# A decoder layer on one core: input projections in native fp32, rotation's angles made first, memory keys and values in three passes of float32r

## The chip, the cores and the metric

The kernel runs on one core of one Trainium2 chip. The metric is device time in microseconds from one launch, lower is better. Three runs of the kernel before took 1092.56, 1095.22 and 1095.38 us (median 1095.22). Its five engines are named as in the profile: PE is TensorE's matmul, PEld its weight load, DVE is VectorE, ACT is ScalarE, POOL is GpSimd, and SP is the engine whose queue issues the loads.

## What is computed

One layer of a decoder on 256 tokens of width 1024, all in float32. Cut to what matters here:

```python
hn   = rmsnorm(x, mix_norm_g)
proj = hn @ w_in                     # 1024 x 2328: conv_a, conv_b, q, six k/v parts, gate logits
y_conv = silu(layernorm(conv31(conv_a * sigmoid(conv_b))))   # 31 taps per channel
q_r, k_s, k_w = partial_rope(...)    # rotation by cos and sin of positions * inv
y_nsa  = gated sum of compressed, selected and window attention
h  = x + concat(y_conv, y_nsa) @ w_out
k, v = rmsnorm(mem) @ w_mem_k, rmsnorm(mem) @ w_mem_v        # 256 memory rows
h  = h + softmax_attention(rmsnorm(h) @ w_mem_q, k, v) @ w_mem_o
h  = h + peer(rmsnorm(h))            # 16384 experts, top 16 of each of 8 heads
out = rmsnorm(h, final_norm_g)
```

## The kernel before

**Two ways to multiply float32.** In the first (`mm3`, lines 147 to 150) both operands are split into a high part of type float32r and the rest, also float32r, and three matmuls are summed: high by high, high by low, low by high. A weight chunk of 128 by 1024 is loaded into a `raw` buffer (`wload`, four buffers) and split there by `wsplit`: two ACT copies `hi` of 128x512 (line 137) and two DVE subtractions `lo` (line 138), with six `hi` and six `lo` buffers, that is, three chunks' worth. In the second way one matmul reads the float32 operands as they are. It needs no split, and the trace shows it as two matmul records.

**The stages in PE's order.** PE's instructions stand in the order of the program; the other engines' order is made by a planner that takes, at each simulated moment, the earliest instruction of the program that is ready, so that ready work is pulled ahead where an engine would be idle.

1. Input projections of the convolution (lines 286 to 309): for four channel blocks a chunk `pb` and a chunk `pa`, eight contraction steps each, by three float32r passes. `hx_h` and `hx_l` are x times the norm's gain, split. The norm's factor is found beside it: ACT squares, DVE sums (`r0.add`), PE adds over partitions (`ss_x`), DVE makes the inverse root in some 14 small steps, PE spreads it as a row (`sr_x`). Until that row is there, no `pb` or `pa` can be read out, and four PSUM buffers hold them. `conv_in` then makes u, and 31 taps per block (124 in all, line 271 and 273) run on DVE; `conv(n)` puts n of them at a place of the program.
2. The positions are loaded and the angles of the rotation are made: ten steps on DVE (lines 318 to 339), two sines on ACT.
3. Two chunks `pkv`, six chunks `pq` (with the rotation, one small permuting matmul `rp` each), and four chunks `pv` of 280 columns (lines 345 to 421). The memory's rows are loaded, scaled (`mg`, line 367), and their norm is made.
4. Attention (lines 471 to 668). Sixteen units of scores, softmax and transposes stand in PE's order with a filler between them: `fill(n)` takes n steps from a generator that makes the memory's keys (`pmk`, line 442, 64 steps) and values (`pmv`, line 458, 64 steps), each step one native float32 matmul. Before the unit of n = 13 ends, 106 of the 128 steps are used; there PE needs the sum of all convolution outputs (`lsum`, made by DVE after the last tap) for the layer norm's mean, `pmu` (line 619).
5. The output projection, memory attention, the search of the experts, and the two large expert products (from line 673), which the change doesn't touch.

Of the kernel before, what the change touches and what calls it, by code (L numbers as in the profile page):

```python
# [9 lines left out]
F32 = mybir.dt.float32  # L10
# [23 lines left out]
_n = 0  # L34
for _name, _w in (("mix_g", 8), ("memq_g", 8), ("memkv_g", 8), ("peer_g", 8), ("conv_w", 4 * TAPS),
                  ("conv_b", 4), ("ln_g", 4), ("ln_b", 4), ("cmp_b1", 2), ("cmp_b2k", 1),
                  ("cmp_b2v", 64), ("cmp_pos", 32)):
    PC[_name] = (_n, _n + _w)
    _n += _w
NPAR = _n  # L40
# [1 line left out]
CC = {}  # L42
_n = 0
for _name, _w in (("ident", 128), ("iota", 128), ("iota16", 16), ("perm", 128), ("causal", 128), ("cmp_add", 32),
                  ("cmp_mul", 32), ("rsel", 512), ("inv", 1), ("sgn", 1)):
    CC[_name] = (_n, _n + _w)
    _n += _w
NCON = _n
# [3 lines left out]
def constants():  # L52
    c = np.zeros((P, NCON), np.float32)

    def put(name, v):
        a, b = CC[name]
        c[:, a:b] = v

    p = np.arange(P)
    put("ident", np.eye(P))  # L60
    d = p % 64
    sw = np.where(d < 8, p + 8, p - 8)
    perm = np.zeros((P, P), np.float32)
# [22 lines left out]
    inv = (np.float32(500000.0) ** (-(np.arange(8, dtype=np.float32) * np.float32(2.0) / np.float32(16.0)))).astype(np.float32)  # L86
    put("inv", np.where(d < 16, inv[d % 8], 0.0)[:, None])
    put("sgn", np.where(d < 8, -1.0, np.where(d < 16, 1.0, 0.0))[:, None])
    put("iota16", np.broadcast_to(cc[None, :], (P, 16)))
    return c  # L90


def build(tc, A, out, dbg=None):
# [19 lines left out]
    def Pm(name):  # L113
        return par[:, PC[name][0]:PC[name][1]]
# [123 lines left out]
    nc.sync.dma_start(xT[:, 0:2], A["xT"][:, 0:2])  # L238
    nc.sync.dma_start(par, A["par"])
    w0 = wload(A["w_in_t"][0])  # L240
    for q in range(1, 4):
        nc.sync.dma_start(xT[:, 2 * q:2 * q + 2], A["xT"][:, 2 * q:2 * q + 2])


    hx_h = h2p.tile([P, KC, T], F32R, name="hx_h", tag="act_h")
    hx_l = h2p.tile([P, KC, T], F32R, name="hx_l", tag="act_l")
    hx = (hx_h, hx_l)
    r0 = Rstd("x", pool=ch, eng=V)
    w0 = wsplit(w0)
    for k in range(KC):  # L250
        g = Pm("mix_g")[:, k:k + 1]
        if k in (1, 2, 3, 4, 5, 6, 7):
            S.activation(hx_h[:, k], xT[:, k], AF.Copy, scale=g)
        else:
            V.tensor_scalar(hx_h[:, k], xT[:, k], g, None, op0=ALU.mult)
        V.scalar_tensor_tensor(hx_l[:, k], xT[:, k], g, hx_h[:, k].bitcast(F32), op0=ALU.mult, op1=ALU.subtract)


    u = ch.tile([P, 4, 30 + T], F32, name="u")
# [26 lines left out]
    pend = []  # L286
    for i in range(4):
        pb = psum(T, f"pb{i}")
        wb = wchunk(A["w_in_t"][2 * i]) if i else w0
        proj(pb, wb, hx, range(4))  # L290
        if i == 1:
            r0.sums()
        proj(pb, wb, hx, range(4, KC))
        wa = wchunk(A["w_in_t"][2 * i + 1], None)
        if i == 0:
            for k in range(KC):
                r0.add(xT[:, k])
# [13 lines left out]
    posi = wk.tile([P, T], I32, name="posi", tag="rt")  # L311
    nc.sync.dma_start(posi, A["pos"].partition_broadcast(P))


    Ct = ch.tile([P, T], F32, name="Ct")
    St = ch.tile([P, T], F32, name="St")
    posf = wk.tile([P, T], F32, name="posf", tag="tb")
    V.tensor_copy(posf, posi)
    ang = wk.tile([P, T], F32, name="ang", tag="th")
    V.tensor_scalar(ang, posf, C("inv"), None, op0=ALU.mult)  # L320
    kk = wk.tile([P, T], F32, name="kk", tag="ta")
    MAGIC = 12582912.0
    V.tensor_scalar(kk, ang, 1.0 / (2.0 * math.pi), None, op0=ALU.mult)
    V.tensor_scalar(kk, kk, MAGIC, None, op0=ALU.add)
    V.tensor_scalar(kk, kk, MAGIC, None, op0=ALU.subtract)
    c1 = 6.28125
    c2 = float((np.array([2.0 * math.pi - c1], np.float32).view(np.uint32) & np.uint32(0xFFFFF000)).view(np.float32)[0])
    c3 = 2.0 * math.pi - c1 - c2
    for c in (c1, c2, c3):
        V.scalar_tensor_tensor(ang, kk, -c, ang, op0=ALU.mult, op1=ALU.add)  # L330
    PIF = 3.1415925
    V.tensor_scalar(ang, ang, PIF, -PIF, op0=ALU.min, op1=ALU.max)
    halfpi = cst.tile([P, 1], F32, name="halfpi")
    V.memset(halfpi, math.pi / 2)
# [778 lines left out]
def layout(inp):  # L1113
# [11 lines left out]
        np.broadcast_to(b2[1][None, :], (P, 64)), pos_l], axis=1))  # L1125
# [48 lines left out]
```

## Time and profile before

| | before |
|---|---|
| median of three runs | 1095.22 us |
| the profiled execution's own time | 1095.67 us |
| its span, first to last instruction | 1093.9 us |
| outside the span | 1.8 us |
| granted TensorE clock, mean of the span | 0.990 |
| busy: PE, PEld, DVE, ACT, POOL | 1066.3, 980.1, 877.1, 587.6, 102.0 us |

Matmuls overlap in the pipeline, so a busy PE is read by the distance between starts and not by the duration of one record. In the table of windows the columns are: stretch in us, its length, then for PE, PEld, DVE, ACT and POOL the busy time with the number of instructions, then the granted clock (1.00 is 2.4 GHz, half of it 1.2 GHz), the share of the DMA engines and GB/s. In a timeline they are start, duration, engine, line, operation, output and inputs, shapes, count, and in brackets the idle time before it and what ended that.

### The profile page before, as it was taken

The numbers are of one execution on the slowest core, as the hardware profiler recorded it, in microseconds if no ns is written. First come the engines' busy times: TensorE is split into PE (matmuls) and PEld (weight loads), VectorE is DVE, ScalarE is ACT, GpSimd is POOL, SyncE is SP. The second block draws the span as 40 slices with busy tenths as digits, with TensorE's granted clock in tenths as the row PEclk, the third lists the DMA queues.
The fourth block names the chain that finished last, engine by engine and source line by source line (L and its number), as shares of the span: only waits on it lengthen the run. The fifth ranks groups of instructions, "written<-read, shape, count | busy, mean of one in ns | idle before, by whom it ended". The sixth has DMA issues, their size and how long they took to land.

```text
span 1093.9 us, 20604 instructions
## 1 busy us (share of the span) xinstructions
PE 1066.3 (97%) x7361; PEld 980.1 (90%) x7362; DVE 877.1 (80%) x2229; ACT 587.6 (54%) x1349; POOL 102.0 (9%) x82
## 2 busy tenths in 40 slices
PE   8889999999999999999999999999999999999997
PEld 7878878999999999999999999998888888888885
DVE  6998956988779999788899999996666666666665
ACT  5731446656445555665555555455555555555554
POOL 0000000000027994000000000001000000000000
PEclk9899999999999999999999999999999999999999
DMA  8633224644444564555544455456665665555652
GB/s 272 215 100 106 88 78 135 203 144 136 155 154 139 171 198 147 184 167 160 167 158 155 158 169 157 155 182 206 194 196 195 193 195 193 195 194 193 194 192 79
DMA packets 51687, 182.47 MB, mean 167 GB/s; under 512 B 5760, under 2 KB 6528, under 8 KB 51456
## 3 DMA queue, kind: packets, MB, share of 16 engines
q1 hardware_dynamic: 51296, 180.62, 50.7%
q8 instruction: 58, 0.95, 0.4%
q10 hardware_dynamic: 288, 0.52, 0.1%
q14 instruction: 45, 0.37, 0.1%
HBM read 179.81 MB, written 1.05 MB: 165 GB/s over the span
## 4 chain that ended last, share of the span: by engine, by line
PE 83%; DVE 14%; ACT 1%; issue 1%; DMA 1%; SPq 0%; ACTq 0%; DVEq 0%
PE Y L1074 32%; PE pu L148 9%; PE pu L150 8%; PE pu L149 8%; PE pmk L442 3%; PE pmv L458 2%; PE pw L1020 1%; PE ppq L148 1%; PE ppq L149 1%; PE ppq L150 1%; PE pw L1021 1%; DVE lo L138 1%; DVE ohx L951 1%; DVE ohx L949 1%; PE pmw L149 1%; PE pmw L148 1%
## 5 line engine op out<-in xcount | busy, mean ns | idle before, releaser
L137 ACT ACTIVATE hi<-raw 128x512 fp32r<-128x512 f32 x632 | 380.1, 624 | 179.0 <-PE pu L149 67.1
L138 DVE TENSOR_TENSOR lo<-raw,hi 128x512 fp32r<-128x512 f32 (+1 forms) x564 | 372.6, 683 | 27.4 <-ACT hi L137 21.5
L148 PE MATMUL pu<-hn_h,hi 128*128 128x256 f32 x1024 | 296.0, 289 | 0.0
L150 PE MATMUL pu<-hn_h,lo 128*128 128x256 f32 x1024 | 290.4, 284 | 1.9 <-DVE lo L138 1.9
L149 PE MATMUL pu<-hn_l,hi 128*128 128x256 f32 x1024 | 290.3, 284 | 0.0
L150 PEld LDWEIGHTS pu<-hn_h,lo 128*128 128x128 f32 x1024 | 197.0, 192 | 2.1 <-DVE lo L138 2.1
L149 PEld LDWEIGHTS pu<-hn_l,hi 128*128 128x128 f32 x1024 | 197.2, 193 | 0.0
L148 PEld LDWEIGHTS pu<-hn_h,hi 128*128 128x128 f32 x1024 | 197.1, 192 | 0.0
L1074 PE MATMUL Y<-hi,ah 128*128 128x512 f32 x512 | 158.2, 389 | 0.0
L1074 PE MATMUL Y<-hi,al 128*128 128x512 f32 x512 | 158.1, 389 | 0.0
L1074 PE MATMUL Y<-lo,ah 128*128 128x512 f32 x512 | 158.0, 389 | 0.0
L1074 PEld LDWEIGHTS Y<-lo,ah 128*128 128x128 f32 x512 | 96.1, 188 | 19.9
L1074 PEld LDWEIGHTS Y<-hi,al 128*128 128x128 f32 x512 | 96.1, 188 | 19.9
L1074 PEld LDWEIGHTS Y<-hi,ah 128*128 128x128 f32 x512 | 96.1, 188 | 19.9
L158 DVE TENSOR_TENSOR al<-slB,ah 128x256 fp32r<-128x256 f32 x88 | 37.4, 425 | 86.1 <-PE Y L1074 86.1
L157 ACT ACTIVATE ah<-slB 128x256 fp32r<-128x256 f32 x88 | 36.8, 418 | 110.7 <-PE Y L1074 110.7
L138 POOL TENSOR_TENSOR lo<-raw,hi 128x512 fp32r<-128x512 f32 x68 | 94.5, 1417 | 12.6 <-ACT hi L137 10.1
L1026 ACT ACTIVATE slB<-pw 128x348 f32<-128x348 f32 (+31 forms) x64 | 32.5, 507 | 70.4 <-DVE slB L1025 58.9
L273 DVE SCALAR_TENSOR_TENSOR yc<-u,par,yc 128x256 f32<-128x256 f32 x120 | 56.0, 478 | 0.3
L158 DVE TENSOR_TENSOR al<-slA,ah 128x256 fp32r<-128x256 f32 x40 | 17.6, 440 | 36.9 <-PE Y L1074 36.9
L157 ACT ACTIVATE ah<-slA 128x256 fp32r<-128x256 f32 x40 | 16.7, 418 | 49.3 <-PE Y L1074 48.0
L148 PE MATMUL ppq<-gx_h,hi 128*128 128x256 f32 x128 | 37.3, 292 | 0.0
(387 smaller groups left out, 1768.8 us busy)
## 6 DMA issues: line engine op xcount, KB each, us to landing
raw<-u SPq DMA_DIRECT2D x128, 512.0 KB, 3.4
raw<-v SPq DMA_DIRECT2D x128, 512.0 KB, 4.3
raw<-peer_w_q SPq DMA_DIRECT2D x16, 512.0 KB, 3.4
raw<-w_in_t SPq DMA_DIRECT2D x15, 512.0 KB, 4.6
raw<-w_mem_k SPq DMA_DIRECT2D x8, 512.0 KB, 3.5
raw<-w_mem_v SPq DMA_DIRECT2D x8, 512.0 KB, 3.4
raw<-w_out SPq DMA_DIRECT2D x8, 512.0 KB, 3.8
raw<-w_mem_q SPq DMA_DIRECT2D x8, 512.0 KB, 4.3
```

Source lines behind the costliest of these rows:

```text
L137: S.activation(hi, r, AF.Copy)
L138: (engs or (V, V))[q].tensor_sub(lo, r, hi.bitcast(F32))
L148: PE.matmul(ps, w[0], xh, start=start, stop=False)
L149: PE.matmul(ps, w[0], xl, start=False, stop=False)
L150: PE.matmul(ps, w[1], xh, start=False, stop=stop)
L157: S.activation(dst[0], src, AF.Copy)
L158: V.tensor_sub(dst[1], src, dst[0].bitcast(F32))
L273: V.scalar_tensor_tensor(yc[:, i], u[:, i, j:j + T], w, yc[:, i], op0=ALU.mult, op1=ALU.add)
L442: PE.matmul(ps, wr[:, k * P:(k + 1) * P], mg[:, k], start=(k == 0), stop=(k == KC - 1))
L458: PE.matmul(pss[hf], mg[:, k, sl], wr[:, j * 256:(j + 1) * 256], start=(k == 0), stop=(k == KC - 1))
L1026: S.activation(slB[:, done - J:, n0:n0 + 4].rearrange("p i n -> p n i"), pw[:, :, done:], AF.Copy, scale=1.0 / GSC)
L1074: PE.matmul(Y[nh][c], lhs[:, sl], wc[c][t], start=False, stop=i == KEYS - 1 and lhs is a[1], skip_group_check=True)
```

## The change

The sixteen input chunks and the four `pv` chunks are multiplied in native float32 from the raw weights and one tile `hx` (no `hx_l`, no split of these weights). The angles' constants move to the parameters that are loaded first, the load of the positions moves ahead of the rest of x in SP's queue, and the angles are made on DVE ahead of the convolution, with one multiply-and-add fused and the sign put into the sine's scale; the two sines stay behind the loop over the blocks. The memory's keys and values are multiplied in three float32r passes, with split weights and a split `mg`. The place of `r0.rows()` moves from behind six contraction steps of `pa` to behind four.

```diff
+    def proj1(ps, w, x, ks=range(KC)):
+        for k in ks:
+            PE.matmul(ps, w[0][:, k * P:(k + 1) * P], x[:, k], start=k == 0, stop=k == KC - 1)
...
+    posi = wk.tile([P, T], I32, name="posi", tag="rt")
+    nc.sync.dma_start(posi, A["pos"].partition_broadcast(P))
     for q in range(1, 4):
         nc.sync.dma_start(xT[:, 2 * q:2 * q + 2], A["xT"][:, 2 * q:2 * q + 2])
-    hx_h = h2p.tile([P, KC, T], F32R, name="hx_h", tag="act_h")
-    hx_l = h2p.tile([P, KC, T], F32R, name="hx_l", tag="act_l")
+    hx = h2p.tile([P, KC, T], F32, name="hx", tag="act_h")
     for k in range(KC):
-            S.activation(hx_h[:, k], xT[:, k], AF.Copy, scale=g)
...
-        V.scalar_tensor_tensor(hx_l[:, k], xT[:, k], g, hx_h[:, k].bitcast(F32), op0=ALU.mult, op1=ALU.subtract)
+        V.tensor_scalar(hx[:, k], xT[:, k], Pm("mix_g")[:, k:k + 1], None, op0=ALU.mult)
+        r0.add(xT[:, k])
+    V.tensor_copy(posf, posi)
+    V.tensor_scalar(ang, posf, Pm("inv"), None, op0=ALU.mult)
+    V.tensor_scalar(kk, ang, 1.0 / (2.0 * math.pi), MAGIC, op0=ALU.mult, op1=ALU.add)
+    V.tensor_scalar(kk, kk, MAGIC, None, op0=ALU.subtract)
...
+    V.scalar_tensor_tensor(aabs, ang, -1.0, ang, op0=ALU.mult, op1=ALU.max)
...
-        wb = wchunk(A["w_in_t"][2 * i]) if i else w0
-        proj(pb, wb, hx, range(4))
+        wb = wload(A["w_in_t"][2 * i]) if i else w0
+        proj1(pb, wb, hx)
         if i == 1:
             r0.sums()
-        proj(pb, wb, hx, range(4, KC))
-        wa = wchunk(A["w_in_t"][2 * i + 1], None)
+        wa = wload(A["w_in_t"][2 * i + 1])
-        proj(pa, wa, hx, range(6))
+        proj1(pa, wa, hx, range(4))
         if i == 1:
             r0.rows()
...
-    S.activation(St, ang, AF.Sin)
-    V.tensor_scalar(St, St, C("sgn"), None, op0=ALU.mult)
+    S.activation(St, ang, AF.Sin, scale=Pm("sgn"))
+    S.activation(Ct, aabs, AF.Sin, scale=-1.0, bias=halfpi)
-        proj(ps, wchunk(A["w_in_t"][8 + i]), hx)
+        proj1(ps, wload(A["w_in_t"][8 + i]), hx)
...
-        proj(ps, wchunk(A["w_in_t"][10 + i]), hx)
+        proj1(ps, wload(A["w_in_t"][10 + i]), hx)
-    mg = mp.tile([P, KC, T], F32, name="mg", tag="b8c")
+    mg = mp.tile([P, KC, T], F32R, name="mg", tag="b8c")
+    mg_l = mp.tile([P, KC, T], F32R, name="mg_l", tag="b8d")
-        S.activation(mg[:, k], mT[:, k], AF.Copy, scale=Pm("memkv_g")[:, k:k + 1])
+        gain_split(mg[:, k], mg_l[:, k], mT[:, k], Pm("memkv_g")[:, k:k + 1])
-        wc = wsplit(wload(A["w_in_v"][w], 560), (V, V), 280, 280)
+        wc = wload(A["w_in_v"][w], 560)[0]
-            wr = wload(A["w_mem_k"][i])[0]
+            wc = wchunk(A["w_mem_k"][i])
-                PE.matmul(ps, wr[:, k * P:(k + 1) * P], mg[:, k], start=(k == 0), stop=(k == KC - 1))
+                proj(ps, wc, (mg, mg_l), [k])
                 yield
-                wr = wload(A["w_mem_v"][c, w])[0]
+                wc = wchunk(A["w_mem_v"][c, w], width=256)
-                        PE.matmul(pss[hf], mg[:, k, sl], wr[:, j * 256:(j + 1) * 256], start=(k == 0), stop=(k == KC - 1))
+                        PE.matmul(pss[hf], mg[:, k, sl], wc[j][0], start=(k == 0), stop=False)
+                        PE.matmul(pss[hf], mg[:, k, sl], wc[j][1], start=False, stop=False)
+                        PE.matmul(pss[hf], mg_l[:, k, sl], wc[j][0], start=False, stop=(k == KC - 1))
                         yield
```

## Rows read from the trace of the kernel before

**Rows 1.** Windows, the stretches from the start to the output projection.

```profile
0.00:24.90 24.90, 20.31 (x128) 18.89 (x129) 17.23 (x52) 14.29 (x30) 2.30 (x11) 0.98 0.80 259
24.90:38.20 13.30, 13.30 (x104) 13.30 (x104) 12.13 (x30) 10.51 (x25) 0.00 (x0) 0.92 0.87 296
38.20:50.60 12.40, 7.76 (x48) 7.56 (x48) 12.02 (x32) 8.34 (x15) 0.00 (x0) 0.74 0.50 182
50.60:74.60 24.00, 21.59 (x159) 20.87 (x158) 21.62 (x64) 8.79 (x19) 0.00 (x0) 0.92 0.35 98
74.60:85.25 10.65, 8.53 (x58) 7.46 (x57) 10.65 (x31) 2.82 (x8) 0.00 (x0) 1.00 0.48 149
85.25:165.30 80.05, 80.05 (x450) 65.83 (x449) 59.45 (x200) 30.32 (x110) 0.00 (x0) 1.00 0.27 87
165.30:188.30 23.00, 22.00 (x133) 17.75 (x131) 17.28 (x57) 14.53 (x42) 0.00 (x0) 1.00 0.48 159
```

**Rows 2.** Waits of PE in 0 to 86 us: total, times, longest.

```profile
PE pkv L150 <- DVE lo L138: 4.6, 1, 4.6
PE pq L150 <- DVE lo L138: 2.4, 2, 2.0
PE pv L415 <- DVE lo L138: 2.1, 4, 1.0
PE sr_x L224 <- DVE dg_x L218: 2.0, 1, 2.0
```

**Rows 3.** Timeline of PE: single steps of each kind of matmul.

```profile
12.27 0.39 PE L148 MATMUL pa<-hx_h,hi 128*128 128x256 f32 x1
...
14.05 0.28 PE L148 MATMUL pa<-hx_h,hi 128*128 128x256 f32 x1
14.41 0.28 PE L148 MATMUL pa<-hx_h,hi 128*128 128x256 f32 x1
...
45.92 0.58 PE L150 MATMUL pkv<-hx_h,lo 128*128 128x256 f32 x1 [4.64 <-DVE lo L138]
46.30 0.41 PE L148 MATMUL pkv<-hx_h,hi 128*128 128x256 f32 x1
...
46.94 0.41 PE L148 MATMUL pkv<-hx_h,hi 128*128 128x256 f32 x1
...
83.87 0.29 PE L414 MATMUL pv<-hi,hx_h 128*128 128x280 f32 x1
...
84.26 0.29 PE L414 MATMUL pv<-hi,hx_h 128*128 128x280 f32 x1
```

**Rows 4.** Chain that ended last, in order of time: start, length, piece.

```profile
105.61 3.08 PE pmk L442 x14
```

**Rows 5.** Timeline of PE around the norm's factor.

```profile
17.39 0.61 PE L209 MATMUL ss_x<-ones,sa_x 128*128 128x1 f32 x4
...
23.67 1.19 PE L224 MATMUL sr_x<-dg_x,ones 128*128 128x128 f32 x4 [1.98 <-DVE dg_x L218]
```

**Rows 6.** Groups of DVE's instructions, 0 to 85.3 us: count, busy us, mean ns.

```profile
L138 DVE TENSOR_TENSOR lo<-raw,hi 128x512 fp32r<-128x512 f32 x32 | 21.7, 684 | 2.2 <-ACT hi L137 2.2
L138 DVE TENSOR_TENSOR lo<-raw,hi 128x280 fp32r<-128x280 f32 x8 | 3.5, 443 | 0.0
L256 DVE SCALAR_TENSOR_TENSOR hx_l<-xT,par,hx_h 128x256 fp32r<-128x256 f32 x8 | 3.5, 481 | 0.2 <-ACT hx_h L253 0.2
L255 DVE TENSOR_SCALAR hx_h<-xT,par 128x256 fp32r<-128x256 f32 x1 | 0.4, 357 | 3.3 <-DMA par<-par 3.3
```

**Rows 7.** The same for 85.3 to 190 us.

```profile
L273 DVE SCALAR_TENSOR_TENSOR yc<-u,par,yc 128x256 f32<-128x256 f32 x70 | 32.1, 478 | 0.3
```

**Rows 8.** Tiles of the layer norm's mean: durations ns, first and last start.

```profile
L613 DVE TENSOR_TENSOR lsum<-lsum,lsum x1: 426/426/426, 145.2 to 145.2; 128x256 f32<-128x256 f32 x1
L619 PE MATMUL pmu<-lsum,ones x2: 379/380/382, 165.3 to 165.6; 128*128 128x256 f32 x2
```

**Rows 9.** Tile of the positions: its load from issue to landing.

```profile
DMA to landing us min/median/max: 7.4/7.4/7.4
```

More of the change, by code (lines that the diff above doesn't have):

```diff
@@ L36 @@
                   ("conv_b", 4), ("ln_g", 4), ("ln_b", 4), ("cmp_b1", 2), ("cmp_b2k", 1),
-                  ("cmp_b2v", 64), ("cmp_pos", 32)):
+                  ("cmp_b2v", 64), ("cmp_pos", 32), ("inv", 1), ("sgn", 1)):
     PC[_name] = (_n, _n + _w)
@@ L44 @@
 for _name, _w in (("ident", 128), ("iota", 128), ("iota16", 16), ("perm", 128), ("causal", 128), ("cmp_add", 32),
-                  ("cmp_mul", 32), ("rsel", 512), ("inv", 1), ("sgn", 1)):
+                  ("cmp_mul", 32), ("rsel", 512)):
     CC[_name] = (_n, _n + _w)
@@ L85, in constants, with rope_constants @@
     put("rsel", rs.reshape(P, 512))
-    inv = (np.float32(500000.0) ** (-(np.arange(8, dtype=np.float32) * np.float32(2.0) / np.float32(16.0)))).astype(np.float32)
-    put("inv", np.where(d < 16, inv[d % 8], 0.0)[:, None])
-    put("sgn", np.where(d < 8, -1.0, np.where(d < 16, 1.0, 0.0))[:, None])
     put("iota16", np.broadcast_to(cc[None, :], (P, 16)))
     return c
+def rope_constants():
+    d = np.arange(P) % 64
+    inv = (np.float32(500000.0) ** (-(np.arange(8, dtype=np.float32) * np.float32(2.0) / np.float32(16.0)))).astype(np.float32)
+    return np.stack([np.where(d < 16, inv[d % 8], 0.0), np.where(d < 8, -1.0, np.where(d < 16, 1.0, 0.0))], axis=1).astype(np.float32)
 def build(tc, A, out, dbg=None):
@@ L240, in build @@
     w0 = wload(A["w_in_t"][0])
+    posi = wk.tile([P, T], I32, name="posi", tag="rt")
+    nc.sync.dma_start(posi, A["pos"].partition_broadcast(P))
     for q in range(1, 4):
         nc.sync.dma_start(xT[:, 2 * q:2 * q + 2], A["xT"][:, 2 * q:2 * q + 2])
-    hx_h = h2p.tile([P, KC, T], F32R, name="hx_h", tag="act_h")
-    hx_l = h2p.tile([P, KC, T], F32R, name="hx_l", tag="act_l")
-    hx = (hx_h, hx_l)
+    hx = h2p.tile([P, KC, T], F32, name="hx", tag="act_h")
     r0 = Rstd("x", pool=ch, eng=V)
-    w0 = wsplit(w0)
     for k in range(KC):
-        g = Pm("mix_g")[:, k:k + 1]
-        if k in (1, 2, 3, 4, 5, 6, 7):
-            S.activation(hx_h[:, k], xT[:, k], AF.Copy, scale=g)
-        else:
-            V.tensor_scalar(hx_h[:, k], xT[:, k], g, None, op0=ALU.mult)
-        V.scalar_tensor_tensor(hx_l[:, k], xT[:, k], g, hx_h[:, k].bitcast(F32), op0=ALU.mult, op1=ALU.subtract)
+        V.tensor_scalar(hx[:, k], xT[:, k], Pm("mix_g")[:, k:k + 1], None, op0=ALU.mult)
+        r0.add(xT[:, k])
+    posf = wk.tile([P, T], F32, name="posf", tag="tb")
+    V.tensor_copy(posf, posi)
+    ang = St = ch.tile([P, T], F32, name="St")
+    V.tensor_scalar(ang, posf, Pm("inv"), None, op0=ALU.mult)
+    kk = wk.tile([P, T], F32, name="kk", tag="ta")
+    MAGIC = 12582912.0
+    V.tensor_scalar(kk, ang, 1.0 / (2.0 * math.pi), MAGIC, op0=ALU.mult, op1=ALU.add)
+    V.tensor_scalar(kk, kk, MAGIC, None, op0=ALU.subtract)
+    c1 = 6.28125
+    c2 = float((np.array([2.0 * math.pi - c1], np.float32).view(np.uint32) & np.uint32(0xFFFFF000)).view(np.float32)[0])
+    c3 = 2.0 * math.pi - c1 - c2
+    for c in (c1, c2, c3):
+        V.scalar_tensor_tensor(ang, kk, -c, ang, op0=ALU.mult, op1=ALU.add)
+    PIF = 3.1415925
+    V.tensor_scalar(ang, ang, PIF, -PIF, op0=ALU.min, op1=ALU.max)
+    aabs = Ct = ch.tile([P, T], F32, name="Ct")
+    V.scalar_tensor_tensor(aabs, ang, -1.0, ang, op0=ALU.mult, op1=ALU.max)
+    halfpi = cst.tile([P, 1], F32, name="halfpi")
+    V.memset(halfpi, math.pi / 2)
     u = ch.tile([P, 4, 30 + T], F32, name="u")
@@ L288, in build @@
         pb = psum(T, f"pb{i}")
-        wb = wchunk(A["w_in_t"][2 * i]) if i else w0
-        proj(pb, wb, hx, range(4))
+        wb = wload(A["w_in_t"][2 * i]) if i else w0
+        proj1(pb, wb, hx)
         if i == 1:
             r0.sums()
-        proj(pb, wb, hx, range(4, KC))
-        wa = wchunk(A["w_in_t"][2 * i + 1], None)
+        wa = wload(A["w_in_t"][2 * i + 1])
         if i == 0:
-            for k in range(KC):
-                r0.add(xT[:, k])
             nc.sync.dma_start(con1, A["con"][:, 0:NCON1])
         pa = psum(T, f"pa{i}")
-        proj(pa, wa, hx, range(6))
+        proj1(pa, wa, hx, range(4))
         if i == 1:
@@ L303, in build @@
             conv_in(*pend)
-        proj(pa, wa, hx, range(6, KC))
+        proj1(pa, wa, hx, range(4, KC))
         if i == 0:
@@ L310, in build @@
     nc.sync.dma_start(con2, A["con"][:, NCON1:])
[L311 to L334, printed above, removed]
-    S.activation(St, ang, AF.Sin)
-    V.scalar_tensor_tensor(kk, ang, -1.0, ang, op0=ALU.mult, op1=ALU.max)
-    S.activation(Ct, kk, AF.Sin, scale=-1.0, bias=halfpi)
+    S.activation(St, ang, AF.Sin, scale=Pm("sgn"))
+    S.activation(Ct, aabs, AF.Sin, scale=-1.0, bias=halfpi)
     S.activation(halfpi, Ct[:, 0:1], AF.Tanh)
-    V.tensor_scalar(St, St, C("sgn"), None, op0=ALU.mult)
     KV = [ch.tile([P, 3, 272], F32, name=f"KV{i}", tag=f"nsa{i}") for i in range(2)]
@@ L413, in build @@
                 sl = slice(hf * P, (hf + 1) * P)
-                PE.matmul(pv[hf], hx_h[:, k, sl], wc[j][0], start=(k == 0), stop=False)
-                PE.matmul(pv[hf], hx_h[:, k, sl], wc[j][1], start=False, stop=False)
-                PE.matmul(pv[hf], hx_l[:, k, sl], wc[j][0], start=False, stop=(k == KC - 1))
+                PE.matmul(pv[hf], hx[:, k, sl], wc[:, j * 280:(j + 1) * 280], start=(k == 0), stop=(k == KC - 1))
         if w % 2:
@@ L1124, in layout @@
         a["cmp_b1"][0].T, np.concatenate([b2[0], b2[0]])[:, None],
-        np.broadcast_to(b2[1][None, :], (P, 64)), pos_l], axis=1))
+        np.broadcast_to(b2[1][None, :], (P, 64)), pos_l, rope_constants()], axis=1))
     o["pos"] = a["positions"][0]
```

## The prediction, made before the changed kernel was run

> **What bounds the kernel now.** I read the windows by stage first, then PE's waits, then single steps in PE's timeline, then the groups of DVE. Two stages are touched, and they have different limits.
>
> The input projections end at 85.25 us. The reader is to see in the windows that DVE is nearly full there (12.02 of 12.40 us, 21.62 of 24.00, 10.65 of 10.65) while PE is not (7.76 of 12.40) [rows 1], and in the list of waits what PE stood for: 9.1 us for the low halves of split weights (4.6 + 2.4 + 2.1), and 2.0 for the norm's factor [rows 2]. After the longest wait a contraction step of three passes takes 46.94 - 46.30 = 0.64 us, where it took 14.41 - 14.05 = 0.36 earlier [rows 3]; the granted clock is 0.74 of full in that stretch against 1.00 elsewhere [rows 1], so a wait is paid about twice.
>
> The attention with its filler, 85.25 to 165.30 us, is the other way round: PE is busy for all of 80.05 us at clock 1.00, DVE 59.45 and ACT 30.32 [rows 1]. Only fewer PE cycles can shorten it. From 165.30 to 188.30 PE is busy 22.00 of 23.00 [rows 1], with less room in its waits for the layer norm. What follows has the same instructions in the same order in both kernels, so I carry a shift over unchanged.
>
> **Prices.** A three-pass step of 256 columns costs 0.36 us at full clock [rows 3]. A native step costs 3.08 / 7 = 0.44 (two records a step) [rows 4]. For 280 columns three passes cost 84.26 - 83.87 = 0.39 [rows 3]; native is not shown, and 0.44 x 280 / 256 = 0.48 is my estimate. So native costs PE 0.08 more a step (0.09 at 280 columns), and three passes in the filler 0.08 less.
>
> The Trainium skill, in "FP8 and Floating Point Precision", section "TensorE Precision Notes", counts true float32 as four passes, which makes a native step 4/3 of three passes, 0.48 us as an estimate. The trace doesn't agree: the ratio is 0.44 / 0.36 = 1.22. By the page's price the front would be some 5.5 us longer than I make it and the filler some 4 us shorter before the mean, about 1084 us in all; the row decides.
>
> **Front: the sum.** The first `pa` step starts at 12.27 [rows 3]. I keep that point: the changed kernel needs no split before its first chunk, but its eight `hx` and eight sums stand on DVE in pairs of 0.36 + about 0.4 us behind the arriving x, and eight such pairs cover what the split cost. The positions' load, now ahead of most of x in SP's queue, is 128 KB; it landed 7.4 us after issue in the crowd [rows 9]. Its bounds are nothing and a quarter of a chunk's time of 2 to 3 us; I take it inside the kept point. Then:
>
> - `pa0` and `pb1`, 16 steps of 0.44: 7.0, to 19.3. The norm's sum follows, and four more steps carry PE to 21.6.
> - The chain from that sum to the row took 23.67 - 17.39 = 6.28 us [rows 5], with splits of 0.68 [rows 6] between its small steps. Those are gone; the angles' steps may take their place. Bounds are 6.28 and 6.28 less five splits, 2.9; I take 4.0, nearer the low end. PE then waits 1.8 us (2.0 before [rows 2]) and is past the row at 24.2.
> - 36 steps to the end of `pa3`: 15.8, to 40.0. `pkv`, 16 steps: 7.0, to 47.1. `pq`, 48 steps: 21.1, to 68.2. `pv`, 16 steps of 0.48: 7.7, to 75.9.
> - Six small permuting matmuls of 0.44: 2.6. The memory norm's two small groups, priced by those of rows 5 (0.61 and 1.19, less at full clock): 1.3, to 79.8.
> - Low clock after the one wait left: the stretch behind it had 0.92 over 13.30 us [rows 1], that is up to 1.06 us lost; I take 0.5.
>
> The front ends at 80.3 instead of 85.25: **5.0 us saved**, bounds 0 (another feeder takes the place of the splits) and 7.3 (no wait, no low clock: 80.3 - 1.8 - 0.5 = 78.0). Without the splits the angles' DVE work and the table switch for the sines hide behind PE's steps, since the sines are first needed by the rotation behind `pq2`; the 4.64 us in front of `pkv`, where one `lo` stood behind this work, have nothing left to stop. What is late next is the norm's factor.
>
> The loads. Each raw buffer is now held until PE has read it, about 3.5 us, and SP's queue, in order, also carries the copies of `kvT`, which wait for PE and DVE. Four buffers give some 10 us of lead against a load's few; I cost that at nothing and keep up to 5 us for the range.
>
> **Filler: the sum.** Before the mean's matmul PE takes 106 of 128 steps: 106 x 0.08 = **8.5 us saved**. The remaining 22 save 1.8, but there PE soon waits for the layer norm's chain as it did (1.0 us of 23.00 [rows 1]); I keep 0.7.
>
> This stage now needs splits. ACT gets 32 copies, some 20 us, beside 30.32 + 14.53 busy of 103 [rows 1]: hidden. DVE is the question. Up to the mean it was busy 17.23 + 12.13 + 12.02 + 21.62 + 10.65 + 59.45 = 133.1 us [rows 1]. It loses 21.7 + 3.5 + 3.5 = 28.7, gains 7 x 0.36 = 2.5 for `hx` and 8 x 0.48 = 3.9 for the low half of `mg` [rows 6], and 14 chunks x 2 x 0.68 = 19.0 of splits. That is 129.8 us, in 80.3 + 71.5 = 151.8 us up to the mean instead of 165.3. Its sum of taps was ready at 145.6 for a use at 165.3 [rows 8], so it was 20 us ahead; now it is about level. It works out only if taps are pulled into the front: the front frees 28.7 - 6.4 = 22.3 us. If all of it is filled with taps (70 of them, 32.1 us, stood in the filler's stage [rows 7]), the stage holds 59.45 + 19.0 - 22.3 = 56.2 us of DVE work in 71.5, and nothing is felt. If none is, it holds 78.5, and with DVE's own waits as before (80.05 - 59.45 = 20.6) 99.1: 27.5 us too long. Taps are ready from the first `conv_in` on, and the planner takes whatever is ready, so I stand near the low end and take 1.5 us, as small waits at chunk borders and before the mean.
>
> **The total.** 5.0 + 8.5 - 1.5 + 0.7 = 12.7 us. The profiled execution took 1095.67 us (1093.9 of span and 1.8 around it): 1083.0. It is 0.45 above the median of the runs, so I predict **1082.5 us**.
>
> **The rivals.**
>
> *All covered (1077.7 us).* The factor's chain shrinks so far that PE doesn't wait, and DVE is never felt: 7.3 + 8.5 + 1.8 = 17.6. For it: DVE's total falls by 3.3 us. Against it: even the shortest chain, 2.9 us, is longer than the four steps behind the sum (1.8).
>
> *The front stays as long (1087.5 us).* Loads held back by the raw buffers, or the norm's chain at its old 6.28 us behind the angles' steps, take the 5.0 us; the filler's part stays. For it: DMA was 0.80 to 0.87 busy up to 38 us [rows 1]. Against it: native steps want a chunk only every 3.5 us, where three passes wanted one every 2.9.
>
> *Passes alone decide (about 1097 us).* The front's 11 us of waits come back under other names, so that PE pays 128 x 0.08 + 16 x 0.09 = 11.7 more there and gets 128 x 0.08 = 10.2 back later: 1.5 slower, no change that can be measured. Against it: 9.1 of the 11 us are waits for an instruction that is gone [rows 2].
>
> *DVE becomes the bound of the filler (up to 1108 us, slower).* Taps are not pulled ahead, PE waits before the mean: 5.0 saved, 99.1 - 80.05 = 19.1 lost, 1.8 saved in the tail, 1095.2 + 12.3 = 1107.5. It is felt from 71.5 us of DVE work and waits in that stage, and makes the kernel slower than before from about 86. For it: the small distance, 129.8 of 151.8 us. Against it: DVE was as full (0.9 and more) in the front before and still ended 20 us early.
>
> **How the numbers follow.** Chances: forecast 0.45, all covered 0.23, front as long 0.15, passes alone 0.08, DVE the bound 0.09. The likeliest's own range is 1078 to 1088. For 8 in 10 the range takes in both neighbours and part of the DVE case: 1074 to 1095. About 0.3% (3.3 us) is what a measurement can tell from no change. Faster than that holds in the first three cases, 0.83; no change in passes alone, 0.07; slower 0.10.
>
> **What would show it.** Right: the first memory-key step starts near 80 us; PE's waits for `lo` in the front are gone and one wait of 1 to 2.5 us for the factor is left; native input steps stand 0.44 apart and the filler's 0.36; the mean's matmul is at 150 to 154. Wrong: the clock in the front stays below 0.95, PE waits for loads there, or in the filler's stage PE waits for `lo` or for the sum of taps by more than 4 us in all.

## The result, and the profile after

The changed kernel takes 1082.98 us (median of 4 runs, 1082.72 to 1084.66), the kernel before 1094.97 on the same chip (1092.56 to 1095.38). The ratio is 0.9899, interval 0.9883 to 0.9915: 12 us faster. The forecast was 1082.5. The profiled execution took 1082.72 us with a span of 1080.9; the one of before 1095.67 with 1093.9.

Where the time came from is read off the first start of one tile per stage (us, tile view of both kernels; the shift is after minus before):

```
stage's first matmul            before   after   shift
pa    second input chunk          12.3    14.4    +2.1
sr_x  norm's factor as a row      23.7    24.5    +0.8
pkv   keys and values             38.0    40.6    +2.6
pq    queries                     50.8    47.5    -3.3
pv    values                      74.6    70.4    -4.2
pmk   memory keys (filler)        85.5    79.1    -6.4
pmu   layer norm's mean          165.3   152.6   -12.7
pwo   output projection          183.3   170.4   -12.9
Y     last stage                 737.8   724.8   -13.0
```

The front loses 2.6 us up to `pkv`, then gains 9.0; the filler up to the mean gains 6.3; behind the mean next to nothing changes. The windows by stage of the changed kernel (columns: stretch, length, busy us of PE, weight loads, DVE, ACT and POOL with counts, granted clock, DMA share, GB/s) answer to [rows 1]:

```profile
0.00:24.90 24.90, 20.89 (x91) 18.32 (x92) 11.02 (x48) 9.28 (x17) 2.30 (x11) 0.93 0.74 241
24.90:40.60 15.70, 15.70 (x75) 13.87 (x75) 15.41 (x42) 7.03 (x18) 0.00 (x0) 1.00 0.90 313
40.60:47.50 6.90, 6.90 (x33) 6.09 (x32) 6.90 (x20) 0.83 (x2) 0.00 (x0) 1.00 0.57 165
47.50:70.40 22.90, 22.90 (x109) 20.24 (x108) 22.90 (x74) 2.08 (x5) 0.00 (x0) 1.00 0.40 115
70.40:79.00 8.60, 8.60 (x40) 7.09 (x39) 8.36 (x22) 2.26 (x5) 0.00 (x0) 1.00 0.62 182
79.00:152.60 73.60, 72.56 (x556) 64.29 (x556) 63.73 (x201) 46.80 (x143) 0.00 (x0) 1.00 0.36 119
152.60:175.30 22.70, 20.36 (x152) 17.44 (x152) 17.53 (x58) 13.98 (x40) 0.00 (x0) 1.00 0.22 70
```

From 24.9 to 79 us PE now has no gap, and its clock is 1.00 in every one of these stretches; before it was busy 7.76 of 12.40 in one of them, at 0.74 [rows 1]. PE's waits from 0 to 190 us (waiting line, line waited for: total us, times, longest) answer to [rows 2]:

```profile
PE sr_c L233 <- DVE dg_c L227: 2.3, 1, 2.3
PE pb L163 <- DVE hx L259: 2.1, 1, 2.1
PE pmu L616 <- DVE asm L565: 1.1, 1, 1.1
PE sr_x L233 <- DVE dg_x L227: 0.9, 1, 0.9
```

All three waits for `lo` are gone and the factor's wait is halved. At the start one wait of 2.1 us for `hx` stands where three of 0.7, 0.3 and 0.3 stood. The wait for the layer norm's row (`sr_c`) grew from 1.0 to 2.3, and one of 1.1 at the mean is new. Its row names `asm`, but `pmu` doesn't read that; it reads the sum of taps, which ended 0.1 us before (below). DVE's timeline (start, length, instruction, idle time before it and its end) shows what stood in front of `hx`, and ACT's, whose queue holds none of the angles' steps there, when x's second part could be used:

```profile
8.67 0.29 DVE L264 CAST posf<-posi 128x256 f32<-128x256 int32 x1 [3.35 <-DMA posi<-pos]
9.00 0.35 DVE L266 TENSOR_SCALAR St<-posf,par 128x256 f32<-128x256 f32 x1
9.39 0.29 DVE L269 TENSOR_SCALAR kk<-St 128x256 f32<-128x256 f32 x1
9.60 0.61 DVE L259 TENSOR_SCALAR hx<-xT,par 128x256 f32<-128x256 f32 x2
```

```profile
9.57 0.72 ACT L210 ACTIVATE sq_x<-xT 128x256 f32<-128x256 f32 x2 [5.08 <-DMA xT<-xT]
```

The angles' first steps waited 3.35 us for the positions, which were loaded ahead of x, and went first on DVE. They held `hx` up by next to nothing: ACT waited for x itself until 9.57, and `hx` began at 9.60. What came late is x, behind the positions' load. PE ran again from 10.00, and the windows of those 4.4 us show a clock of 0.61:

```profile
8.00:10.00 2.00, 0.00 (x0) 0.00 (x1) 1.26 (x5) 0.43 (x2) 0.00 (x0) 1.00 1.03 369
10.00:14.40 4.40, 4.40 (x13) 3.65 (x14) 4.37 (x16) 3.25 (x6) 0.00 (x0) 0.61 0.80 322
```

A native step in an unbroken run, from PE's timeline: 16 records from 66.52 to 69.97, so 3.45 / 8 = 0.431 us a step.

```profile
66.52 3.62 PE L163 MATMUL pq<-hx,raw 128*128 128x256 f32 x16
69.97 0.59 PE L376 MATMUL rp<-qraw,con 128*128 128x256 f32 x2
```

Seven three-pass steps of the filler in the chain that ended last (start, length, piece): 111.74 to 114.32, 2.58 us, where seven native ones took 3.08 [rows 4].

```profile
111.74 0.17 PE pmk L152
111.92 0.12 PE pmk L153
...
112.16 0.12 PE pmk L152
...
114.19 0.12 PE pmk L154
114.32 0.44 PE ptt L581 x4
```

And the sum of taps against the mean's matmul (tile view: durations, first to last start), which answers to [rows 8]:

```profile
L616 PE MATMUL pmu<-lsum,ones x2: 380/418/455, 152.6 to 152.9; 128*128 128x256 f32 x2
L610 DVE TENSOR_TENSOR lsum<-lsum,lsum x1: 417/417/417, 152.1 to 152.1; 128x256 f32<-128x256 f32 x1
```

It ends at 152.5 for a use at 152.6, where it was 20 us early before: DVE and PE now reach the mean together.

### The profile page after: what moved, and what is told of

Its sections match the earlier page's. It is cut to its first block, busy times and chain, and to the rows that moved or that the text cites. A ratio compares the mean times of both kernels' runs of the same rounds, so it can differ in the third digit from the quotient of the medians.

```text
span 1080.9 us, 20534 instructions
## 1 busy us (share of the span) xinstructions
PE 1061.2 (98%) x7346; PEld 976.3 (90%) x7346; DVE 871.8 (81%) x2226; ACT 580.0 (54%) x1334; POOL 102.3 (9%) x82
## 4 chain that ended last, share of the span: by engine, by line
PE 85%; DVE 13%; ACT 1%; DMA 1%; issue 0%; SPq 0%; DVEq 0%; ACTq 0%
PE Y L1071 32%; PE pu L152 9%; PE pu L154 8%; PE pu L153 8%; PE pq L163 2%; PE pw L1017 1%; PE ppq L152 1%; PE ppq L153 1%; PE ppq L154 1%; PE pb L163 1%; PE pw L1018 1%; PE pa L163 1%; DVE ohx L948 1%; PE pmk L152 1%; DVE lo L142 1%; DVE ohx L946 1%
## 5 line engine op out<-in xcount | busy, mean ns | idle before, releaser
L142 DVE TENSOR_TENSOR lo<-raw,hi 128x512 fp32r<-128x512 f32 x556 | 369.1, 687 | 26.8 <-ACT hi L141 21.0
L142 POOL TENSOR_TENSOR lo<-raw,hi 128x512 fp32r<-128x512 f32 x68 | 94.8, 1421 | 11.8 <-ACT hi L141 9.2
```

The lines of the kernel that those rows point to most:

```text
L142: (engs or (V, V))[q].tensor_sub(lo, r, hi.bitcast(F32))
```

## The experiments

The change has three parts: the native front (F), the early angles (A) and the three-pass memory projections (M). Every kernel below was timed against the kernel before on its own chip; the medians of before lay between 1094.37 and 1095.01 us. The kernels with late angles, F alone and M alone among them, already have the angles' constants among the first parameters and two DVE steps fewer; what that does by itself was not run.

**F alone.** The front of the changed kernel in the kernel before.

```diff
-    hx_h, hx_l = ...            # split of x
-        proj(pb, wchunk(A["w_in_t"][2 * i]), hx, ...)
+    hx = h2p.tile([P, KC, T], F32, name="hx", tag="act_h")
+        proj1(pb, wload(A["w_in_t"][2 * i]), hx)
...
```

> Only the input projections go native; the angles stay where they were and the memory's projections stay native float32. Theory (the splits' low halves and the work in front of them on VectorE were what TensorE waited for in the front; native steps have nothing to wait for): the front's 6.4 us are gained here too, 1088 to 1090 us, first memory-key step at 78 to 80 us. Rival (the early angles are what removed the 4.6 us wait before pkv): only 1 to 2 us gained, 1093 to 1094.

Measured: 1085.75 us (1084.99 to 1087.31), ratio 0.9921 (0.9909 to 0.9934). `pmk` starts at 77.4 and the mean at 157.2, so the front gains 8.1 us and the native filler takes the 79.8 us that it took before. The sum of taps is done at 108.0, 49 us ahead. The front by itself is worth more than the 5.0 us of the prediction's term, and more than I expected here.

**A alone.** Positions and angles moved ahead, the splits of the front kept.

```diff
+    posi = ...; nc.sync.dma_start(posi, ...)      # ahead of x's other parts
+    posf, St, kk, ..., Ct                         # ahead of the projections
...
-    posi, posf, St, kk, ..., Ct                   # behind the convolution's inputs
```

> Only the positions' load and the angles are moved to the start; all splits stay as before. Theory: the wait before pkv is cut, but the positions' load ahead of x costs some 2 us at the start, and other low halves are late: 1092 to 1095 us. Rival (angles are the main part): 1089 to 1091.

Measured: 1096.41 us (1094.14 to 1098.45), ratio 1.0016 (1.0007 to 1.0025). The 4.6 us in front of `pkv` are gone, and PE waits 5.6 for `lo` at `pq` instead (2.4 before [rows 2]), 2.8 for the factor (2.0) and 2.1 at `pb`. With the splits in place the wait only changes its name. The time lies above my range; the trace doesn't show why, since its filler starts 0.7 us earlier than before (84.8).

**M alone.**

```diff
-            wr = wload(A["w_mem_k"][i])[0]
-                PE.matmul(ps, wr[...], mg[:, k], ...)
+            wc = wchunk(A["w_mem_k"][i])
+                proj(ps, wc, (mg, mg_l), [k])
...
```

> Only the memory's key and value projections go to three passes; input projections and angles as before. Theory (the filler's splits can only be paid with VectorE time that the front's native projections set free): VectorE is the bound of the filler, TensorE waits for the sum of the taps before the mean's matmul, 1094 to 1104 us, no gain. Rival (the parts add up): the 6.4 us of the filler are gained here too, 1087 to 1090.

Measured: 1102.62 us (1102.05 to 1107.33), ratio 1.0079 (1.0064 to 1.0093): slower. PE's waits in this kernel, among them:

```profile
PE pq L154 <- DVE lo L142: 4.4, 2, 3.8
PE pkv L154 <- DVE lo L142: 3.8, 1, 3.8
PE pmu L628 <- DVE lsum L622: 3.5, 1, 3.5
PE pmv L466 <- DVE lo L142: 3.4, 3, 1.3
PE pmk L154 <- DVE lo L142: 3.2, 3, 2.1
```

The last three stand in the filler's stage and make 10.1 us. The clock from 85.5 to 171 us is 0.98, another 1.7. The cheaper steps give 7.5 back (106 x 0.071, below), which leaves 4.3 of the 5.9 us by which the mean is later (171.2 for 165.3); 1.6 I cannot place. Behind the mean the clock is 0.56 from 171.2 to 178 us, and `pwo` starts 8.1 us later than before (191.4). This is the prediction's DVE rival, and without the front's relief it happens.

**F and M, the angles late.** The changed kernel with the positions and angles where they were.

```diff
-    posi, posf, St, kk, ..., Ct                   # ahead of the projections
...
+    posi, posf, St, kk, ..., Ct                   # behind them, as before
```

> The changed kernel with the positions' load and the angles back behind the convolution's loop. Theory: the native projections have no need of the early angles, and the start is freed of the positions' load: 1080.5 to 1083.5 us, TensorE's wait of 2.1 us in the first chunk gone. Rival (the early angles are a main part): 1086 to 1089.

Measured: 1087.39 us (1087.19 to 1088.76), ratio 0.9936 (0.9923 to 0.9949). I had expected this kernel to lose nothing, and this theory fell. Its front is indeed shorter (`pmk` at 76.9), but at the mean PE stands for the taps, and the window behind that wait shows the clock:

```profile
PE pmu L616 <- DVE lsum L610: 4.0, 1, 4.0
```

```profile
153.50:157.00 3.50, 3.50 (x14) 2.63 (x15) 2.83 (x10) 1.50 (x4) 0.00 (x0) 0.52 0.47 160
```

The 4.0 us cost another 1.7 in clock (0.48 of 3.50), where the changed kernel has 1.00 behind its 1.1 us wait. Its last sum of taps starts at 152.9, the changed kernel's at 152.1 although all else there is 2.2 us later. The mean itself is only 0.9 us later than in the changed kernel (153.5), `pwo` 3.6 (174.0): most of the loss lies behind the wait, where the clock is 0.60 again from 170.0 to 173.5. The early angles use DVE time that is idle otherwise (before 24.9 us DVE is busy 11.02 us in the changed kernel, 9.43 here), and that time is missing later: by 79 us DVE has done 71 taps of the later kind here, 77 in the changed kernel.

**F and A, the memory native.**

```diff
-            wc = wchunk(A["w_mem_k"][i])
-                proj(ps, wc, (mg, mg_l), [k])
+            wr = wload(A["w_mem_k"][i])[0]
+                PE.matmul(ps, wr[...], mg[:, k], ...)
...
```

> The changed kernel with the memory's projections back in native float32 (native front and early angles kept). Theory (early angles pay only where VectorE is the bound of the filler; here it is not): they only cost the late start, 1086 to 1088.5 us, slower than the native front alone (1085.75). Rival (early angles are worth their 4.4 us in any kernel): 1080 to 1082.

Measured: 1089.62 us (1088.61 to 1090.34), ratio 0.9953 (0.9939 to 0.9966). The sum of taps is done at 102.9, `pa` starts at 13.6, the mean is at 158.4. It is slower than F alone by 0.0032, as I expected, and just above my range. On this footing M is worth 0.9953 - 0.9899 = 0.0054, 5.9 us.

**A and M, the front split.** The last cell.

```diff
-    hx = h2p.tile([P, KC, T], F32, name="hx", tag="act_h")
-        proj1(pb, wload(A["w_in_t"][2 * i]), hx)
+    hx_h, hx_l = ...
+        proj(pb, wchunk(A["w_in_t"][2 * i]), hx, ...)
...
```

> Early angles and three-pass memory, but input projections in three passes as before. Theory (the filler's splits need the VectorE time that only the native front sets free): no better than the memory alone (1102.6), 1098 to 1105 us, with waits for low halves in the filler and for the sum of the taps at the mean. Rival (early angles free enough of VectorE): 1088 to 1096.

Measured: 1104.16 us (1102.66 to 1105.38), ratio 1.0090 (1.0076 to 1.0104), as expected. Its longest waits:

```profile
PE pq L154 <- DVE lo L142: 7.4, 2, 6.9
PE pmu L628 <- DVE lsum L622: 3.5, 1, 3.5
PE pmv L466 <- DVE lo L142: 3.4, 3, 1.3
```

The eight cells as ratios to before (0.001 is 1.1 us):

```
               angles late   angles early
split front
  memory native     1           1.0016
  memory 3-pass     1.0079      1.0090
native front
  memory native     0.9921      0.9953
  memory 3-pass     0.9936      0.9899
```

So M costs 0.0079 alone, 0.0074 with A, 0.0015 with F (the two intervals overlap, so this one may be nothing), and gains 0.0054 with F and A. A costs 0.0016 alone and 0.0032 with F, and gains 0.0037 with F and M; its 0.0011 with M is within the intervals. Only F gains in every row. What A and M have in common is DVE's time before the mean: M spends it, F supplies it, and A adds to it where F is in place.

**Half of the splits on GpSimd.** The changed kernel with one of a memory chunk's two `lo` on GpSimd.

```diff
-            wc = wchunk(A["w_mem_k"][i])
+            wc = wchunk(A["w_mem_k"][i], (V, G))
...
```

> The changed kernel with the second of the two low halves of each memory chunk made on GpSimd, which is idle there, so that VectorE has some 11 us less to do before the mean. Theory (VectorE is the bound at the mean and behind it): TensorE's wait of 1.1 us at the mean goes, the one of 2.3 us before the layer norm's row shrinks, 1079.5 to 1082 us. Rival (VectorE is level but does not bind, or GpSimd's 1.4 us halves come late): 1083 to 1087, with waits for low halves in the filler.

Measured: 1084.22 us (1082.77 to 1084.86), ratio 0.9905 (0.9890 to 0.9920). The sum of taps is ready at 138.3, 14 us ahead, and the mean is at 152.6 all the same; my expectation was too fast. The wait of 1.1 us went, and waits of 1.0 (for `amx`) and 0.4 (for `pcT`) came, in a stage that began 0.6 us earlier. The experiment on GpSimd below shows one reason.

**The positions behind x.** The changed kernel with the positions' load moved behind the last part of x.

```diff
-    posi = wk.tile([P, T], I32, name="posi", tag="rt")
-    nc.sync.dma_start(posi, A["pos"].partition_broadcast(P))
     for q in range(1, 4):
         nc.sync.dma_start(xT[:, 2 * q:2 * q + 2], ...)
+    posi = wk.tile([P, T], I32, name="posi", tag="rt")
+    nc.sync.dma_start(posi, A["pos"].partition_broadcast(P))
```

> The changed kernel with the positions' load behind the last part of x in the queue. Theory: the first pa step is back at 12.3 us instead of 14.4; because VectorE binds at the mean, only part of the 2 us arrives at the end: 1081 to 1083 us. Rival (the start carries over whole): 1080 to 1081.

Measured: 1080.67 us (1079.33 to 1081.19), ratio 0.9868 (0.9853 to 0.9883). `pa` starts at 11.8 instead of 14.4, and 2.4 us of it arrive at the mean (150.2) and at `pwo` (168.0), as the rival had it: DVE starts earlier too. The windows of the start:

```profile
8.00:10.00 2.00, 1.51 (x7) 1.03 (x7) 1.92 (x7) 1.48 (x4) 0.00 (x0) 1.00 0.96 158
10.00:14.40 4.40, 4.40 (x19) 3.15 (x19) 4.23 (x15) 2.20 (x4) 0.00 (x0) 1.00 1.03 406
```

PE still waits for `hx`, 1.7 us instead of 2.1, but the clock stays at 1.00 where it was 0.61. In PE's timeline the twelve matmuls behind the wait begin at 8.49 instead of 10.00 and take 3.3 us to `pa` instead of 4.4: 1.5 us are the earlier end of the wait, 1.1 the clock. The wait ends earlier because x does: ACT goes on with x's second part at 8.08 instead of 9.57, and DVE's `hx` starts at the same moment.

```profile
8.08 0.72 ACT L210 ACTIVATE sq_x<-xT 128x256 f32<-128x256 f32 x2 [3.76 <-DMA xT<-xT]
```

The clock's part doesn't follow from the load. F and A, and the kernel with half of the splits on GpSimd, start like the changed kernel: ACT's wait for x ends at 9.77 and 10.18, PE waits 3.2 and 3.1 us, longer than there, and yet the clock behind stays at 1.00 and `pa` starts at 13.6 and 13.8. The lines of F and A:

```profile
PE pb L163 <- DVE hx L259: 3.2, 1, 3.2
```

```profile
10.46:13.65 3.19, 3.19 (x13) 2.06 (x14) 3.19 (x12) 2.09 (x6) 0.00 (x0) 1.00 0.93 376
```

**Both of these.** Positions behind x and half of the splits on GpSimd.

```diff
-    nc.sync.dma_start(posi, ...)                  # ahead of x's other parts
+    nc.sync.dma_start(posi, ...)                  # behind them
-            wc = wchunk(A["w_mem_k"][i])
+            wc = wchunk(A["w_mem_k"][i], (V, G))
...
```

> Both: positions behind x, second low halves on GpSimd. Theory: with VectorE relieved the 2 us of the start are kept whole and add up with the relief: 1077.5 to 1080 us. Rival (either of the two is worth nothing): 1081 to 1084.

Measured: 1081.05 us (1080.74 to 1081.62), ratio 0.9876 (0.9861 to 0.9891), not to be told from the kernel above. The mean is at 150.1, the sum of taps at 136.4. GpSimd adds nothing here either.

**M alone, all its splits on GpSimd.** If DVE's time were the only trouble of M alone, this would mend it.

```diff
-            wc = wchunk(A["w_mem_k"][i])
+            wc = wchunk(A["w_mem_k"][i], (G, G))
...
```

> The kernel before with the three-pass memory alone, but both low halves of its weights made on GpSimd, so that VectorE has nothing to add but the low half of mg. Theory (the memory change alone was slow for want of VectorE): the filler's 7 us of saved passes appear, 1086 to 1091 us, the mean's sum is ready before TensorE asks. Rival (it was slow for another reason: ACT's copies, the buffers, late halves): 1096 or more, as on VectorE.

Measured: 1106.37 us (1105.04 to 1107.20), ratio 1.0107 (1.0092 to 1.0123), slower than M alone; this theory fell too, though its sum of taps is done 3.6 us ahead of the mean (169.2 for 172.8). Most of the loss stands in front of the filler: `pmk` starts at 90.8 instead of 85.5. There the first splits on GpSimd run beside DVE's last ones for `pv`, which take 576 ns instead of 440, PE waits up to 2.4 us for them, and the clock is 0.50 from 85 to 90 us. From `pmk` to the mean it takes 82.0 us, less than M alone (85.7) and still more than native steps (79.8). From 85.5 to 171 us DVE is busy 83.56 us, against 75.12 in M alone, although 20.8 us of splits are gone from it. The groups of DVE in that stretch (count, busy us, mean ns, idle before), first of M alone:

```profile
L284 DVE SCALAR_TENSOR_TENSOR yc<-u,par,yc 128x256 f32<-128x256 f32 x70 | 32.7, 475 | 0.0
L571 DVE TENSOR_REDUCE amx<-pss 128x2 f32<-128x256 f32 x7 | 2.9, 416 | 1.0 <-PE pss L569 0.9
L583 DVE TENSOR_SCALAR ape<-ape,asm 128x256 f32<-128x256 f32 x14 | 4.5, 345 | 0.0
```

and with GpSimd:

```profile
L284 DVE SCALAR_TENSOR_TENSOR yc<-u,par,yc 128x256 f32<-128x256 f32 x74 | 46.5, 644 | 0.3
L583 DVE TENSOR_SCALAR ape<-ape,asm 128x256 f32<-128x256 f32 x12 | 8.7, 768 | 0.0
L571 DVE TENSOR_REDUCE amx<-pss 128x2 f32<-128x256 f32 x7 | 2.9, 411 | 0.0
```

A tap takes 644 ns instead of 475, the scaling of `ape` 768 instead of 345; the reduction, which reads one operand from PSUM, is unchanged. The timelines of DVE and POOL side by side show one case:

```profile
122.35 2.73 DVE L583 TENSOR_SCALAR ape<-ape,asm 128x256 f32<-128x256 f32 x2
```

```profile
122.36 2.56 POOL L142 TENSOR_TENSOR lo<-raw,hi 128x512 fp32r<-128x512 f32 x2 [2.95 <-ACT hi L141]
```

Two steps of 345 ns stand for 2.73 us beside 2.56 us of GpSimd. The Trainium skill, "SBUF — State Buffer", section "Who interferes with whom", says that DVE instructions with two SBUF inputs or in a two-port mode share a port pair with GpSimd that one of them holds for a whole instruction, and that reductions are exempt. The rows of the tap, which reads two tensors, and of the reduction agree; the scaling's agrees if it ran in a two-port mode, which that section allows it and no row here shows.

**The layer norm two units earlier.** Positions behind x, and the mean, sums and row of the layer norm called two units of the attention earlier, first with the splits on DVE.

```diff
-        if n == 12:
+        if n == 10:
             lsum = ln_mean()
...                                # 13, 15, 16 become 11, 13, 14
```

> The same two units earlier, but all low halves on VectorE. Theory (VectorE is just level at the mean): TensorE now waits 4 to 7 us there for the sum of the taps, 1081 to 1086 us. Rival (VectorE has room): 1076 to 1079.5, as with GpSimd.

Measured: 1087.82 us (1085.61 to 1089.23), ratio 0.9935 (0.9920 to 0.9949). The waits, and the clock behind the first:

```profile
PE pmu L616 <- DVE lsum L610: 5.4, 1, 5.4
PE ptt L581 <- ACT hi L141: 1.8, 1, 1.8
```

```profile
148.70:153.50 4.80, 4.80 (x19) 3.92 (x20) 2.92 (x9) 1.50 (x4) 0.00 (x0) 0.50 0.16 58
153.50:157.00 3.50, 3.50 (x19) 2.71 (x19) 1.46 (x3) 1.60 (x6) 0.00 (x0) 0.70 0.01 2
```

The wait was as long as expected, the time longer: the clock cost 0.50 x 4.80 + 0.30 x 3.50 = 3.5 us more. Against the kernel with the positions behind x that makes 5.4 + 1.8 + 3.5, less its waits of 1.1 and 2.3: 7.3 us, and `pwo` starts 175.2 - 168.0 = 7.2 later. DVE thus has no slack at the mean, as the tile of the sum said.

**The same with half of the splits on GpSimd.**

```diff
-            wc = wchunk(A["w_mem_k"][i])
+            wc = wchunk(A["w_mem_k"][i], (V, G))
-        if n == 12:
+        if n == 10:
...
```

> Positions behind x, second low halves on GpSimd, and the layer norm's mean, sums and rows two units earlier in TensorE's order (the sum of the taps was ready 14 us ahead there). Theory: the wait of 2.2 us before the norm's row and part of the wait for its output go, 1076 to 1079.5 us. Rival (these waits only move): 1080.5 to 1082.

Measured: 1078.67 us (1078.01 to 1080.70), ratio 0.9854 (0.9839 to 0.9869), the lowest median of all, and faster than the changed kernel (0.9899, 0.9883 to 0.9915). From the kernel with the positions behind x (0.9868, 0.9853 to 0.9883) the intervals don't tell it apart. PE's waits past 30 us:

```profile
PE ptt L581 <- DVE ape L571: 1.7, 1, 1.7
PE pss L553 <- ACT ape L564: 0.4, 1, 0.4
```

Against the same order with all splits on DVE (0.9935) GpSimd pays, because the order had been drawn closer than DVE alone could keep. The waits at the mean and for the layer norm's row are gone; a new one of 1.7 stands for `ape` at 167.6, where GpSimd has no work and `ape` takes its usual 0.35 us. In this trace, of the longest of the four runs (1080.70), the waits have only moved: `pwo` starts at 168.1, with the positions behind x at 168.0. That the other runs, 1078.01 to 1079.06, gain from the earlier norm is not shown.

## Why the prediction was right, and where it was not

The time is 0.5 us off and the mechanism held, but that it came so close is partly luck. The start came 2.1 us late, the rest of the front took 3.3 us less than priced, and the filler and the tail gave 1.2 us less. With the start about where the prediction had it, the kernel takes 1080.67 us.

- **The start: wrong.** I kept `pa` at 12.27 and took the positions' load inside it, at most a quarter of a chunk's time (some 0.7 us). It started at 14.37. The load cost more than its bound: x's second part was there at 9.57 with the load ahead of it, at 8.08 with it behind, and 8.35 and 8.64 in F alone and with late angles. The angles' steps that waited on DVE added 0.03 us here and 0.3 in F and A. The rest is the clock, 0.61 behind PE's wait in this trace and 1.00 in the two others with this start. Moving the load gave 2.4 us back.
- **The rest of the front: better than priced.** From `pa` to the filler I had 80.3 - 12.3 = 68.0 us; it took 79.1 - 14.4 = 64.7. The factor's chain took 24.5 - 21.3 = 3.2 us instead of 4.0, so PE waited 0.9 instead of 1.8. The half us for low clock wasn't paid. A native step came 0.431 apart instead of 0.44, some 1.2 us over the 120 steps with the 16 wider ones (75.05 to 78.83, 0.47 each where I estimated 0.48). Some 0.7 us are left to small groups. Together the front saved 6.4 us instead of 5.0, and with the positions moved 8.9 (`pmk` at 76.6). The step "without the splits the angles hide behind PE" was right, and F alone and A alone show that the splits were what stood in the way.
- **The filler's price: too high.** Seven steps save 3.08 - 2.58 = 0.50, so 0.071 a step instead of 0.08: the first matmul of each group takes 0.17 us in the chain instead of 0.12. 106 steps give 7.5 us, not 8.5. The waits cost 1.1 where I put 1.5; 7.5 - 1.1 = 6.4, measured 6.3.
- **DVE level at the mean: right.** The sum of taps ends 0.1 us ahead of its use. Before the filler DVE did 77 taps of the later kind and 4 first ones, where it had done 51 and 3, so 27 taps were pulled ahead, some 13 of the 22.3 us that the front freed. Their groups, in the first 85.3 us before and in the first 79 after:

```profile
L273 DVE SCALAR_TENSOR_TENSOR yc<-u,par,yc 128x256 f32<-128x256 f32 x51 | 24.4, 478 | 0.0
```

```profile
L298 DVE SCALAR_TENSOR_TENSOR yc<-u,par,yc 128x256 f32<-128x256 f32 x77 | 34.4, 472 | 0.0
```

- **The tail: nearly nothing.** I kept 0.7 of 1.8 us; 0.2 came. PE's wait for the layer norm's row grew from 1.0 to 2.3 and took the rest. The kernels in which the norm is called earlier don't have this wait, but one of 1.7 or 1.8 us for other steps.
- **The rivals.** "Passes alone" and "front as long" are out: no wait for `lo` or for a raw buffer is left up to 190 us. "All covered" supposed that DVE is never felt; it is, for 1.1 us. The DVE rival is real but stands one step away: it decides in M alone (1.0079), and in the kernels that take a few us of DVE's lead away (4.0 and 5.4 us of wait). My chance of 0.09 for it rested on the front giving its time to taps, which it did.
- **Carried over unchanged: nearly.** The shift is 12.7 to 13.0 us from the mean to the end here. In F alone it is 8.1 at the mean and 9.9 at the last stage; the 1.8 us arise past 264 us, where nothing was changed, and I have not followed them.
- **Four passes.** The rule of the Trainium skill that the prediction weighs ("FP8 and Floating Point Precision", section "TensorE Precision Notes") gives 4/3 of three passes if a native pass costs as much as a float32r matmul. Within a run the rows give 0.431 to 0.36 (the six steps from 112.16 to 114.32 in the chain, 0.36 each), 1.20. That speaks against the equal price and not against four passes: a quarter of a native step would be 0.108 us at 256 columns and 0.118 at 280, in proportion to the columns, where a float32r matmul takes 0.12 and 0.13.
- **The signs.** `pmk` at 79.1, no wait for `lo`, steps 0.431 and 0.36 apart and the mean at 152.6 are as named. The factor's wait of 0.9 lies just under its 1 to 2.5, and the clock was below 0.95 (0.93) only up to 24.9 us.
- **Two readings were too smooth.** The clock was 0.92 in two more stretches of the front, not 1.00 everywhere else, and DVE was busy 0.69 of the first stretch, not 0.9 [rows 1]. Nor is a wait "paid about twice" in general: 4.0 us cost another 1.7, 5.4 another 3.5, and 1.1 or 2.3 nothing. None of this enters the sum.

Open: half of the splits on GpSimd gave DVE 14 us of lead and PE nothing. Slower DVE steps and 1.4 us of new small waits are seen in that trace; that they are the whole cause is argued, not shown.

## What to carry to other kernels

Price a change of arithmetic by what it takes from and gives to the engine that feeds it: the same three-pass edit cost 0.8% alone and gained 0.5% after two others had freed DVE. When a load is moved ahead of others in a queue, price how much later those arrive: 128 KB ahead of x made x's second part 1.5 us later. To tell a late load from a busy engine, look for a second engine that waits for the same data. A wait of PE is to be read with the clock behind it, from windows, and not by its length alone.

## What the runs showed of the hardware

- Behind waits of PE of 4.0 and 5.4 us the granted clock was 0.52 and 0.50 in the next 3.5 to 4.8 us, half of 2.4 GHz; behind waits of 0.9, 1.1, 1.7 and 2.3 us it stayed at 1.00. The length of the wait alone doesn't decide: behind 2.1 us at the start of the changed kernel it was 0.61 over 4.4 us, behind 3.2 and 3.1 us at the same place in two kernels with the same start 1.00, and behind 2.1 us before the norm's row with F and M alone 0.60 over 3.5, some 13 us after the stretch at 0.52.
- A group of float32r matmuls pays 0.05 us more for its first one (0.17 against 0.12) after the attention's small matmuls.
- GpSimd's subtraction of 128x512 took 1.42 us beside DVE's work, and lengthened DVE's taps by 36% and its two-column scalings from 158 to 324 ns on the mean.
- With the positions' load of 128 KB ahead of x's other parts in SP's queue, ACT could use x's second part at 9.57, 9.77 and 10.18 us in the three kernels with native front and early load; with the load behind it, or late, at 7.95 to 8.75 in six.
